# Token mixers with the dense input products issued two k tiles at a time between the lanes' short products

## The chip, the cores and the metric

The kernel runs on one core of a Trainium2 chip. The metric is the device time of one execution in microseconds (us), the median of several. PE stands for the matrix engine (TensorE), DVE for VectorE, ACT for ScalarE, POOL for GpSimd and SP for SyncE, which here only issues transfers.

## What is computed

Two transformer blocks over 512 tokens of width 1024, in float32. The change touches only the first part of the first block, the token mixers. It projects the normed input with one wide matrix and feeds four kinds of mixer, each with a quarter of the width, whose outputs are joined and projected back:

```python
def token_mix(h, w_in, ...):
    p = (h @ w_in).astype(jnp.float32)
    (fox_qkv, fox_f, gdn_qkv, gdn_b, gdn_a, gdn_z, hg_q, hg_f, hg_i, hg_g,
     gla_qk, gla_v, gla_gk, gla_g) = jnp.split(p, _cut_points(IN_SIZES), axis=-1)
    ...
    o_a = rms_norm(fox_attention(q, k, split_heads(v, FOX_HEADS), log_f), fox_on_g)
    ...
    o_b = gated_delta_chunked(...)      # gated delta rule, state carried from chunk to chunk
    ...
    o_c = gla_chunked(...)              # gated linear attention (hg)
    ...
    o_d = gla_chunked(...)              # gated linear attention (gla)
    ...
    return jnp.concatenate([merge_heads(o_a), merge_heads(o_b), merge_heads(o_c), merge_heads(o_d)], axis=-1)

    # first_block
    mixed = token_mix(rms_norm(x, norm1_g[l]), ...)
    x = x + mixed.astype(x.dtype) @ w_out[l]
```

After it come the first block's feed-forward part and the whole second block (a convolution mixer, a SwiGLU, latent attention, a SwiGLU). They are long chains of dense products, and the change doesn't touch their code.

## The kernel before

Activations lie transposed, as eight tiles of 128 features by 512 tokens. Every dense product is done with operands split into a high and a low part: for each k tile three matmuls of 128x128 by 128x512 (high by high, high by low, low by high), eight k tiles to a product. The weights of one product come in by one transfer of 512 KB; ACT makes the high part (line 111) and DVE the low part (line 112, tile `wl`), in two buffers each.

In the mixers there are two kinds of PE work. The **dense products** are 29 tiles of the input projection and 8 of the output projection (tile `mm` in the rows below, all recorded on line 705, the body of the helper `mm`). The **short products** belong to the mixers, which run as three lanes: `gps` (the gated delta rule: gdn0, then gdn1), `lps` (linear attention: hg0, gla, hg1) and `fps` (attention: fox0, fox1). A lane is a chain: a few short matmuls, then DVE, ACT or POOL work on their result, then the next few short matmuls that need it. Transposes are recorded on line 712.

The order in which PE gets all this is written out when the program is built, by `conduct`, which plays the work through on a clock of its own, `self.clk`. Each matmul moves that clock by an assumed cost (`mm`: 0.216 for a dense one, so 0.648 for a k tile). A lane's generator yields how long it wants to wait before its next step; it is due when the clock has passed that time. In each turn `conduct` takes the first lane that is due, unless a dense product is open and more than `FEED` has passed on the clock since the last dense step; else it takes one step of an open dense product:

```python
if due and not (dense and self.clk - fed > FEED):
```

So with lanes always due, short work for just over `FEED` goes by, then a dense step; with none due, dense steps follow each other until one is due. PE runs the finished order from front to back.

A dense product is opened when the one before it has had its last step, and the next one is chosen at that moment, in the order of `ORDER`, among those whose buffers are free. `over` in `mix` says which part of a lane must have been written out before: the products lf1 and lq1 need `la6.qk`, lv1 needs `la6.v` (both parts of the lane step gla), and hg1 can't start before lf1, lq1 and lv1 are there. The output products come when no input product is left. They need the lanes' outputs as k tiles, and those that lack only the last one are parked until it is there (`parked`). Every product ends on DVE (lines 901, 927, 935 for the input, 859 for the output).

Of the kernel before, what the change touches and what calls it, by code (L numbers as in the profile page):

```python
# [20 lines left out]
KD = D // 128  # L21
# [623 lines left out]

LA, LV, LP = 0.68, 1.0, 1.5

FEED = 1.27

# [12 lines left out]
class Mix(Mla):  # L664
# [55 lines left out]
            self.mm(cols(ps[:, cs]), l[:, cs], cols(r[:, cs]))  # L720
        return ps

    def stepped(self, ws, xs, tag):


        ps = (self.pmm if tag == "mm" else self.psm).tile([128, S], F32, tag=tag, name="mm", bufs=2)
        for k in range(KD):
            while k >= len(xs):
                yield None
            self.step(ps, k, ws[xs[k][0]], xs[k])  # L730
            yield ps, k

    def step(self, ps, k, w, x):
        (h, l), (_, xh, xl) = w, x
# [23 lines left out]
    def conduct(self, jobs, lanes):  # L758
# [8 lines left out]
        first, last = jobs.pop(0), []  # L767
        self.last = last
        xs = [(k, *x) for k, x in enumerate(self.xs)]
        nxt, dense, held = (first, self.first), [], []  # L770
        early = [self.second]
        outs, parked, row = list(range(KD)), [], None
        while True:

            for i, lane in enumerate(lanes):
                if strands[i] is None and lane and all(n in ready for n in lane[0][0]):
                    need, name, gen, rings = lane.pop(0)
                    strands[i] = Strand(gen(), max([self.clk] + [ready[n] for n in need]), rings, name)
            live = self.beside + [s for s in strands if s]
            due = next((s for s in live if s.at <= self.clk), None)  # L780

            while held and "mean" in self.over:
                ps, name, post = held.pop(0)
                t = post(ps)
                if t is not None:
                    ready[name] = max(self.clk, ready["mean"] + C_MEAN) + t
            if nxt is None:
                job = next((j for j in jobs if j[1] in self.over), None)
                if job:
                    jobs.remove(job)  # L790
                    nxt = job, early.pop() if early else self.weight(self.a["w_in"], job[0], KD)
                elif not jobs and outs:
                    c = outs.pop(0)
                    nxt = (c, None, None, self.out_post(c)), self.weight(self.a["w_out"], c, KD)
            if not jobs and not held and all(d[1][2] is None for d in dense) and (not nxt or nxt[0][2] is None):
                while self.ended:
                    p = self.ended.pop(0)
                    last.append((p, *self.parts(self.outs[p], "x", KD)))
                    if len(last) == KD:
                        self.load_x(self.a["xT"])  # L800
                        due_row = self.clk + DUE
            if due and not (dense and self.clk - fed > FEED):
                self.lane = due.rings
                t = next(due.gen, None)
                self.lane = {}
                due.at = self.clk + (t or 0.0)
                if t is None:
                    if due in strands:
                        strands[strands.index(due)] = None
                        self.over.add(due.name)  # L810
                        ready[due.name] = self.clk
                    else:
                        self.beside.remove(due)
                continue
            if not row and len(last) == KD - 1 and not any(lanes) and not any(strands):
                row = self.row_of_out(next(i for i in range(KD) if all(x[0] != i for x in last)))
            if parked and len(last) == KD and row and (self.clk > due_row or not (dense or nxt)):
                ps, c, _ = parked.pop(0)
                self.step(ps, KD - 1, row[c], last[KD - 1])
                held.append((ps, None, self.out_post(c)))  # L820
                fed = self.clk
                continue
            tags = ["mm", *self.idle_psum(lanes, live)] if nxt and nxt[0][2] is None else ["mm"]
            taken = [d[2] for d in dense] + [p[2] for p in parked] + ["mm"] * len(held)
            tag = next((t for t in tags if taken.count(t) < 2), None)
            if nxt and tag and len(dense) + len(held) < 2 and all(d[1][2] is None for d in dense):
                job, ws = nxt
                started += 1
                if started in (3, 4):
                    tag = "fps"  # L830
                dense.append((self.stepped(ws, last if job[2] is None else xs, tag), job, tag))
                nxt = None
                continue
            step = None
            for d in dense:
                step = next(d[0])
                if step:
                    break
            fed = self.clk
            if step:  # L840
                ps, k = step
                if d[1][2] is None and k == KD - 2 and len(last) < KD:
                    dense.remove(d)
                    parked.append((ps, d[1][0], d[2]))
                elif k == KD - 1:
                    dense.remove(d)
                    held.append((ps, *d[1][2:]))
                continue
            if not live:
                assert not jobs and not outs and not dense and not any(lanes) and not held  # L850
                return
            self.clk = max(self.clk, min(s.at for s in live))
# [835 lines left out]
```

## Time and profile before

| | us |
|---|---|
| time, median of 3 runs (1859.42 to 1865.12) | 1862.47 |
| the profiled execution's own time | 1862.47 |
| its span, from the first to the last instruction | 1860.8 |
| PE busy | 1822.3 |
| DVE busy | 1050.7 |
| ACT busy | 737.8 |
| POOL busy | 194.4 |

The busy time of PE is a modelled one: its matmuls are pipelined and overlap in the record, so starts of successive instructions tell more than durations. The mixers take the first 400 us of the span; the last matmul on line 705 starts at 399.3 us. In the timeline, rows of one engine stand in order of their starts, with the time that the engine sat idle before in brackets and what ended it.

### The profile page before, as it was taken

To read this page: it belongs to the slowest core of one execution; us is meant where nothing else is said; L and a number is where in the kernel's file an instruction comes from. 1 tells how busy PE (TensorE), PEld (TensorE's weight loads), DVE (VectorE), ACT (ScalarE), POOL (GpSimd) and SP (SyncE) were. 2 spreads that over 40 slices of the span, in tenths; PEclk is the share of its full clock that TensorE was granted. 3 is DMA by queue.
4 is the path that set the end of the run, shared out by engine and by line. 5 is a ranking of instruction groups with operands and counts; after the bars stand their busy time and mean duration, and the time that the engine had idled before them with its cause. 6 is when DMAs were issued, how large, how long until landed. Compare 5 with 4: busy or idle time off the path is not lost.

```text
span 1860.8 us, 22057 instructions
## 1 busy us (share of the span) xinstructions
PE 1822.3 (98%) x8609; PEld 1501.5 (81%) x8609; DVE 1050.7 (56%) x1627; ACT 737.8 (40%) x1138; POOL 194.4 (10%) x225
## 2 busy tenths in 40 slices
PE   8999999999999999999999999999999999999997
PEld 6787887778888888888888888888777888888886
DVE  7875985767777633455564444333876454444323
ACT  6543544544444422322343233322577333232322
POOL 1510502210000001011200000011011200000001
PEclk9999999999999999999999999999999999999999
DMA  4111101332323333323232323333222222323332
GB/s 167 57 35 46 46 35 35 106 101 91 102 93 100 90 100 94 102 91 102 92 106 92 102 91 102 94 94 97 71 60 74 79 96 97 102 91 99 94 94 76
DMA packets 53223, 162.61 MB, mean 87 GB/s; under 512 B 6528, under 2 KB 13184, under 8 KB 53120
## 3 DMA queue, kind: packets, MB, share of 16 engines
q1 hardware_dynamic: 52992, 161.21, 27.2%
q8 instruction: 67, 1.10, 0.3%
q14 instruction: 36, 0.29, 0.0%
q10 hardware_dynamic: 128, 0.01, 0.0%
HBM read 157.78 MB, written 2.10 MB: 86 GB/s over the span
## 4 chain that ended last, share of the span: by engine, by line
PE 85%; DVE 9%; ACT 3%; issue 1%; POOL 1%; DMA 0%; SPq 0%; DVEq 0%; ACTq 0%; POOLq 0%
PE mm L125 24%; PE mm L127 24%; PE mm L126 24%; PE mm L705 6%; PE gps L705 3%; PE lps L705 1%; PE fps L705 1%; DVE lbd L1310 1%; ACT wh L111 1%; DVE wl L112 1%; DVE lat L1361 1%; PE ps L577 1%; DVE ptl L112 0%; PE ps L165 0%; DVE nm L580 0%
## 5 line engine op out<-in xcount | busy, mean ns | idle before, releaser
L111 ACT ACTIVATE wh<-raw 128x1024 fp32r<-128x1024 f32 (+3 forms) x308 | 308.6, 1003 | 762.6 <-PE mm L126 463.5
L125 PE MATMUL mm<-xh,wh 128*128 128x512 f32 x1336 | 521.8, 391 | 0.4 <-ACT xh L173 0.4
L126 PE MATMUL mm<-xl,wh 128*128 128x512 f32 x1336 | 520.7, 390 | 0.5 <-DVE xl L174 0.5
L127 PE MATMUL mm<-xh,wl 128*128 128x512 f32 x1336 | 519.9, 389 | 0.0
L112 DVE TENSOR_TENSOR wl<-raw,wh 128x1024 fp32r<-128x1024 f32 (+3 forms) x300 | 361.0, 1203 | 224.8 <-ACT wh L111 221.6
L126 PEld LDWEIGHTS mm<-xl,wh 128*128 128x128 f32 x1336 | 250.8, 188 | 54.9 <-DVE xl L174 1.4
L125 PEld LDWEIGHTS mm<-xh,wh 128*128 128x128 f32 x1336 | 250.8, 188 | 53.7 <-issue 1.0
L127 PEld LDWEIGHTS mm<-xh,wl 128*128 128x128 f32 x1336 | 250.8, 188 | 51.9 <-issue 0.2
L125 PE MATMUL mm<-hidh,wh 128*128 128x512 f32 (+1 forms) x614 | 236.7, 386 | 0.0
L127 PE MATMUL mm<-hidh,wl 128*128 128x512 f32 (+1 forms) x614 | 235.3, 384 | 0.0
L126 PE MATMUL mm<-hidl,wh 128*128 128x512 f32 (+1 forms) x614 | 233.8, 381 | 0.0
L127 PEld LDWEIGHTS mm<-hidh,wl 128*128 128x128 f32 x614 | 115.4, 188 | 24.2
L126 PEld LDWEIGHTS mm<-hidl,wh 128*128 128x128 f32 x614 | 115.4, 188 | 23.6
L705 PE MATMUL mm<-xh,wh 128*128 128x512 f32 x291 | 127.7, 439 | 6.6 <-ACT xh L173 5.8
L125 PEld LDWEIGHTS mm<-hidh,wh 128*128 128x128 f32 x614 | 115.5, 188 | 21.9 <-ACT wh L111 0.2
L705 PE MATMUL mm<-xh,wl 128*128 128x512 f32 x291 | 116.0, 398 | 1.6 <-DVE wl L112 1.6
L705 PE MATMUL mm<-xl,wh 128*128 128x512 f32 x291 | 116.1, 399 | 0.4 <-DVE xl L112 0.4
L278 DVE TENSOR_TENSOR u<-mm,rb 128x512 f32<-128x512 f32 x44 | 30.4, 691 | 141.2 <-PE mm L127 141.2
L158 POOL TENSOR_TENSOR z<-z,sq 128x512 f32<-128x512 f32 x31 | 50.9, 1643 | 556.6 <-ACT sq L156 518.9
L274 DVE TENSOR_TENSOR u<-mm,rb 128x512 f32<-128x512 f32 x44 | 30.4, 691 | 90.9 <-PE mm L127 90.8
L111 ACT ACTIVATE hidh<-s 128x512 fp32r<-128x512 f32 x66 | 41.8, 633 | 88.6 <-DVE s L255 57.5
L705 PEld LDWEIGHTS mm<-xh,wh 128*128 128x128 f32 x291 | 56.1, 193 | 18.8 <-ACT xh L173 6.3
(434 smaller groups left out, 2089.2 us busy)
## 6 DMA issues: line engine op xcount, KB each, us to landing
raw<-in_w_a_dram SPq DMA_DIRECT2D x52, 512.0 KB, 3.3
raw<-in_w_b_dram SPq DMA_DIRECT2D x52, 512.0 KB, 3.4
raw<-in_w_up_dram SPq DMA_DIRECT2D x44, 512.0 KB, 3.3
raw<-in_w_in_dram SPq DMA_DIRECT2D x28, 512.0 KB, 3.3
raw<-in_conv_w_in_dram SPq DMA_DIRECT2D x24, 512.0 KB, 3.3
raw<-in_w_down_dram SPq DMA_DIRECT2D x16, 448.0 KB, 3.4
raw<-in_w_a_dram SPq DMA_DIRECT2D x16, 448.0 KB, 3.3
raw<-in_w_b_dram SPq DMA_DIRECT2D x16, 448.0 KB, 3.3
```

The costliest lines, as they stand in the source:

```text
L111: nc.scalar.activation(out=h, in_=src, func=ACTF.Copy)
L112: (eng or nc.vector).tensor_tensor(out=l, in0=src, in1=h.bitcast(F32), op=ALU.subtract)
L125: nc.tensor.matmul(out=ps, lhsT=h, rhs=xh, start=(k == 0), stop=False)
L126: nc.tensor.matmul(out=ps, lhsT=h, rhs=xl, start=False, stop=False)
L127: nc.tensor.matmul(out=ps, lhsT=l, rhs=xh, start=False, stop=(k == kt - 1))
L158: eng.tensor_tensor(out=acc, in0=acc, in1=sq, op=ALU.add)
L274: nc.vector.tensor_tensor(out=g, in0=ps, in1=r, op=ALU.mult)
L278: nc.vector.tensor_tensor(out=g, in0=ps, in1=r, op=ALU.mult)
L577: nc.tensor.matmul(out=ps[:, :n], lhsT=l[:, qs], rhs=r[:, :n], start=(i == 0), stop=False)
L705: self.nc.tensor.matmul(out=out, lhsT=lhsT, rhs=rhs, start=start, stop=stop)
L1310: nc.vector.tensor_tensor(out=bd[rows, :, h].rearrange("p c (n j) -> p c n j", j=b), in0=c4(q)[rows], in1=c4(d)[rows], op=ALU.mult)
L1361: nc.vector.copy_predicated(out=at.rearrange("p c (n j) -> p c n j", j=2 * b)[:, :, :, b:], mask=self.lmask[:, lv - 1].rearrange("p (n j) ...
```

## The change

`stepped`, the generator of one dense product, gets a parameter `many`: it hands back control only after every `many`-th k tile. Input products are made with 2, output products keep 1. `FEED` is doubled. What is computed, the number of instructions, buffers and transfers are the same; the order on PE differs, and with it the moments at which products are opened.

```diff
-FEED = 1.27
+FEED = 2.54
...
-    def stepped(self, ws, xs, tag):
+    def stepped(self, ws, xs, tag, many=1):
...
             self.step(ps, k, ws[xs[k][0]], xs[k])
-            yield ps, k
+            if (k + 1) % many == 0 or k == KD - 1:
+                yield ps, k
...
-                dense.append((self.stepped(ws, last if job[2] is None else xs, tag), job, tag))
+                steps = self.stepped(ws, last, tag) if job[2] is None else self.stepped(ws, xs, tag, 2)
+                dense.append((steps, job, tag))
```

## Rows read from the trace of the kernel before

**Rows 1.** The page: span, engines' busy us, and the granted clock by slices.

```profile
span 1860.8 us, 22057 instructions
PE 1822.3 (98%) x8609; PEld 1501.5 (81%) x8609; DVE 1050.7 (56%) x1627; ACT 737.8 (40%) x1138; POOL 194.4 (10%) x225
PEclk9999999999999999999999999999999999999999
```

**Rows 2.** Busy time of each engine by stretch, with granted clock, DMA share and GB/s.

```profile
120.00:180.00 60.00, 59.38 (x362) 48.60 (x361) 34.61 (x87) 22.52 (x55) 5.26 (x11) 1.00 0.11 36
...
240.00:300.00 60.00, 58.37 (x354) 50.27 (x354) 48.12 (x113) 28.88 (x67) 11.35 (x13) 0.94 0.11 36
...
400.00:1860.00 1460.00, 1443.39 (x6515) 1190.26 (x6514) 757.17 (x998) 542.24 (x758) 96.47 (x115) 1.00 0.29 93
```

**Rows 3.** Timeline of PE: start us, us, engine, line, operation, tiles, shapes, count.

```profile
61.77 0.47 PE L705 MATMUL mm<-xh,wh 128*128 128x512 f32 x1
...
83.04 0.48 PE L705 MATMUL mm<-xh,wh 128*128 128x512 f32 x1
...
83.82 0.53 PE L705 MATMUL gps<-gy,gxt 128*128 128x64 f32 x4
84.18 0.62 PE L705 MATMUL gps<-gxt,gy 128*128 128x64 f32 x4
84.62 0.48 PE L705 MATMUL mm<-xh,wh 128*128 128x512 f32 x1
...
86.10 1.05 PE L705 MATMUL lps<-lbd,lw 128*128 128x128 f32 x8
87.12 0.64 PE L705 MATMUL gps<-gy,gxt 128*128 128x64 f32 x4
87.59 0.62 PE L705 MATMUL gps<-gxt,gy 128*128 128x64 f32 x4
...
335.93 0.48 PE L705 MATMUL mm<-xh,wh 128*128 128x512 f32 x1
```

**Rows 4.** Waits of PE from 60 to 400 us: total us, times, longest.

```profile
PE gps L705 <- DVE gxt L1143: 1.9, 4, 0.6
...
PE gps L705 <- ACT gko L1062: 0.2, 1, 0.2
```

**Rows 5.** Busy time by stretch again, of the two with a lower granted clock.

```profile
110.70:114.10 3.40, 3.40 (x11) 2.83 (x11) 3.37 (x6) 1.78 (x2) 0.00 (x0) 0.50 0.00 0
...
291.60:298.40 6.80, 6.80 (x23) 5.51 (x24) 4.73 (x8) 5.70 (x8) 4.59 (x4) 0.50 0.25 78
```

**Rows 6.** Timeline of PE where the clock fell.

```profile
108.75 0.63 PE L705 MATMUL gps<-gy,gxt 128*128 128x64 f32 x4 [0.96 <-DVE gx L1141]
109.75 0.52 PE L705 MATMUL gps<-gxt,gy 128*128 128x64 f32 x3 [0.36 <-DVE gxt L1143]
...
290.36 0.63 PE L705 MATMUL gps<-gy,gxt 128*128 128x64 f32 x4 [0.53 <-DVE gx L1141]
291.60 1.06 PE L705 MATMUL gps<-gxt,gy 128*128 128x64 f32 x4 [0.60 <-DVE gxt L1143]
292.47 0.77 PE L705 MATMUL mm<-xh,wh 128*128 128x512 f32 x1
```

**Rows 7.** Timelines of PE and DVE: the last linear-attention lane's start and end.

```profile
248.20 0.69 DVE L901 TENSOR_TENSOR fv<-mm,rb 128x512 f32<-128x512 f32 x1 [0.31 <-PE mm L705]
...
276.81 0.69 DVE L901 TENSOR_TENSOR lf<-mm,rb 128x512 f32<-128x512 f32 x1 [0.35 <-PE mm L705]
...
314.76 0.69 DVE L901 TENSOR_TENSOR lv<-mm,rb 128x512 f32<-128x512 f32 x1
...
316.06 0.61 PE L712 MATMUL lps<-mlac,lv 128*128 128x128 f32 x4
...
379.18 0.60 PE L712 MATMUL lps<-mlac,s 128*128 128x128 f32 x4
```

**Rows 8.** Line 705 by tiles: duration ns min/median/max, first and last start us, forms.

```profile
L705 PE MATMUL mm<-xh,wl x291: 387/393/632, 7.2 to 399.3; 128*128 128x512 f32 x146
```

## The prediction

> **What bounds the kernel now.** I read the page first. PE is busy for 1822.3 of 1860.8 us [rows 1], so everything hangs on PE. But that busy time is modelled, and it doesn't tell stages apart. So the busy times by stretch come next. Behind 400 us the code is untouched and PE holds its full clock for 1460 us [rows 2]; I take that part over as it is. All that can move lies in the first 400 us, the mixers, where the clock is at 1.00 in some stretches and at 0.94 in another [rows 2]. There the timeline of PE shows how dense steps (`mm`) and short groups alternate [rows 3], the list of waits shows what PE stood still for [rows 4], and the stretches with a lower clock [rows 5] and what stood ahead of them [rows 6] show the rest.
>
> The reader should see a small pool. The change alters the order of PE's instructions, not their number. PE's idle time between 60 and 400 us comes to 10.0 us in eleven kinds, 15 times in all, from 1.9 us down to 0.2 us (the first and the last of them stand in [rows 4]). The clock stands at 0.50, 1.2 GHz, for 3.4 and for 6.8 us [rows 5], which costs half of that, 5.1 us. An order without any fault could therefore win 15 us, 0.8%, and an order that switches more cheaply a little beside. The other direction has no such bound.
>
> **The change part by part.** The profiled execution took 1862.47 us, exactly the median of the runs shown, with a span of 1860.8 us; sums are made on 1862.5.
>
> **Fewer, longer dense bursts.** Between 60 and 340 us I count 102 bursts of dense steps: 61 of a single k tile (the first at 61.77, the last at 335.93), 36 of two (as at 84.62), five longer [rows 3]. So many are pairs already. A single one takes 0.78 us to the next group (83.04 to 83.82), a pair 1.48 us (84.62 to 86.10) [rows 3]. Two singles made one pair save 1.56 - 1.48 = 0.08 us. That looks like 30 x 0.08 = 2.4 us for the 61 singles. But the short groups pay it back. The group gps<-gy,gxt of four takes 0.36 us where it follows a dense step (83.82 to 84.18; 15 places alike) and 0.47 us where it follows another short group (87.12 to 87.59; the middle of nine places is 0.45) [rows 3]. A merge makes one short group follow a short group instead of a dense step: +0.09. What a switch costs is a cost behind every short group, whatever follows. Bounds: -2.4 us if the short groups pay nothing, +0.3 us if each pays 0.09. I take 0, since the most frequent kind of group shows the payment.
>
> **The feed threshold.** While lanes are always due, short work runs until the planner's clock has passed `FEED`. By `mm` a lane's step counts 0.32 (four of 0.08) up to 1.73 (eight of 0.216), so the threshold is overshot by about 0.45. Before, 0.648 of dense work came for 1.72 of short, 27%; after, 1.296 for 2.99, 30%. Input products go about a tenth faster there and lanes 4% slower. That costs nothing while both kinds are there to fill PE. Output products, with `many` at 1, get half the rate while a lane is due, which also costs nothing as long as the lane fills PE.
>
> **Waits on the lanes.** Where no lane is due at first, a lane that becomes due inside a pair is served up to one k tile (0.70 us, 1.48 - 0.78) later. Its DVE result is older by then, and waits get shorter. Where lanes press, the opposite holds: of two dense steps that lay between short groups one is gone from its place. A lane's matmul whose DVE result isn't there stops PE, and the dense steps queued behind it, on which nothing is missing, wait with it: the group at 291.60 stood idle for 0.60 us, and the dense step behind it began at 292.47 [rows 6]. The trace of before doesn't show such places after the change. Bounds: -10.0 us (every wait gone [rows 4]), and +23 us (30 merges, each uncovering a whole 0.78 us). I take 0, nearest to the pattern of [rows 3], where short groups already stand three in a row (86.10, 87.12, 87.59) without an idle mark; cover is moved from one gap to the next, not removed.
>
> The page "TensorE: Matmul & The Clock Gate" of the Trainium skill says in Part 2 that only weight loads are pulled ahead and that matmuls stay in program order. The trace agrees (292.47 behind 291.60), and this rule speaks against the change.
>
> **Granted clock.** Both falls to 1.2 GHz came right behind two waits on the same lane: 0.96 and 0.36 us ahead of the first, 0.53 and 0.60 us ahead of the second [rows 6]. A new order can lose these two (-5.1 us) or have another like the longer (+3.4 us). I take 0. Single dense steps alone don't bring the clock down: 120 to 180 us holds many and is at 1.00 [rows 2].
>
> The page "Perfetto Trace Analysis" of the Trainium skill, section Matmul Optimizations, says that the engine scales its power with utilization, so that matmuls should run back to back in batches. By that rule pairs should keep the clock up and the 5.1 us would be won; the trace shows the falls behind waits and not behind singles, so the rule has no term in the sum.
>
> **The tail.** hg1 is the last lane. It begins at 316.06, right behind the end of its last input product (lv1, at 314.76), and its last transposes stand at 379.18 [rows 7]. The last dense matmul of the mixers starts at 399.3 [rows 8], 20 us behind that. Of that, the code makes at least the last k tiles of six parked products and two whole products wait for hg1: 6 + 16 = 22 steps of 0.70, 15.4 us. So about 5 us of slack cover a later end of hg1. Cost 0, and with that cover gone each us later is a us lost.
>
> **Transfers and splits.** SP's weight loads, ACT's and DVE's splits and the evacuations keep number and size. They move only with the moments at which products open, a k tile or two. Nothing is moved past another kind of work. Cost 0.
>
> Sum: 1862.5 + 0 + 0 + 0 + 0 + 0 = 1862.5 us.
>
> **The rivals.** A, slower: PE waits more. At the 30 places where a dense step leaves its gap, the lane's result comes too late by half a step: 30 x 0.39 = 11.7 us, 1874 us; with one more fall of the clock 1878. It decides from about 14 such places on (14 x 0.39 = 5.5 us). For it: the planner counts a float32 group of eight as 1.73, while it takes at most 1.02 us (86.10 to 87.12 [rows 3]), so a lane that looks due after 1.0 on that clock has had less time in truth, and without a dense step between nothing makes it up. Against it: three lanes take turns.
>
> B, faster: the two pairs of waits (1.32 and 1.13 us [rows 6]) and both falls (5.1 us [rows 5]) vanish because PE has two k tiles of cover at these places: 7.5 us, 1855.0 us; if short groups don't pay back the 2.4 us, 1852.6. For it: both places had a single step or a pair just behind which the lane wasn't ready. Against it: other such places can arise.
>
> C, slower: hg1 starts one product later. Products are chosen when the one before has ended. lf1, which hg1 needs, was chosen about 248.2, when fv1 ended [rows 7], and became free (la6.qk) only shortly before. If lanes are 4% slower by then, the choice misses it and another product goes first. From lf1's end to lv1's end two products take 38 us (276.81 to 314.76 [rows 7]), 19 each. 19, less 5 for faster products, less 5 of slack, is 9 us: 1872. Against it: the moments of choice move too, and may fall as well.
>
> D: it hardly does what it says, as pairs were there already and output products stay single: 1862, no change.
>
> **How the numbers follow.** A measurement of this kernel can tell about 0.3%, 5.6 us. Forecast (no change) 0.50, D 0.05, A 0.17, C 0.11, B 0.17. Within 0.3%: 0.55. Slower: A and C, 0.28. Faster: B, 0.17. The range goes from 1854 (B, short of its end) to 1875 (C and A, short of A's end), and leaves out some 0.07 below and 0.1 above; the likeliest case by itself spans 1857 to 1868.
>
> **What would show it.** Right, step by step: far fewer single bursts and about 70 to 85 bursts in place of 102; a pair still at 1.48 us and gps<-gy,gxt still at 0.36 and 0.45; waits of PE between 60 and 400 us within 5 us of 10.0; one to three falls of the clock; hg1's last transposes before about 384; from the mixers' end on the same length as before. Wrong: waits above 20 us would be A, waits near 3 us with no fall B, lv1's end behind 325 us C, single bursts as many as before D.

## The result, and the profile after

The changed kernel took 1885.63 us (median of four executions, 1879.77 to 1892.15), the kernel before, run beside it, 1863.24 us. The ratio is 1.0128, with an interval of 1.0111 to 1.0145: slower by 1.3%, where no change was forecast and the range ended at 1875. One execution of the kernel e1 further down took 3070.01 us at a mean granted clock of 0.554, against 0.981 to 0.988 in the others, and is left out of its row.

The page of after: span, engines' busy us, and the granted clock in 40 slices.

```profile
span 1888.6 us, 22059 instructions
PE 1838.6 (97%) x8609; PEld 1516.4 (80%) x8609; DVE 1051.1 (56%) x1627; ACT 739.5 (39%) x1138; POOL 193.0 (10%) x225
PEclk9999997999999999999999999999999999999999
```

The counts of PE's, DVE's, ACT's and POOL's instructions are those of [rows 1], and DVE and ACT are as busy as before. New is the 7 in PEclk. To see which part of the span grew, take the row of the first matmul behind the mixers: its first and last start, before and then after.

```profile
L125 PE MATMUL mm<-xh,wh x1336: 387/389/799, 399.5 to 1725.6; 128*128 128x512 f32 x191
```

```profile
L125 PE MATMUL mm<-xh,wh x1336: 387/389/799, 429.6 to 1753.5; 128*128 128x512 f32 x191
```

The mixers end 30.1 us later (399.5 to 429.6). From there to the span's end it is 1461.3 us before and 1459.0 after. So the whole loss lies in the mixers. Next, busy time by stretch: length, busy PE, PEld, DVE, ACT, POOL, then granted clock. Before, then after:

```profile
60.00:400.00 340.00, 329.74 (x1888) 273.55 (x1887) 247.03 (x533) 154.98 (x311) 88.65 (x88) 0.98 0.17 54
```

```profile
60.00:430.00 370.00, 346.66 (x1885) 288.89 (x1884) 249.46 (x534) 156.53 (x311) 87.31 (x88) 0.93 0.16 51
120.00:180.00 60.00, 58.63 (x373) 49.65 (x372) 31.08 (x72) 20.78 (x50) 4.73 (x9) 1.00 0.11 37
240.00:300.00 60.00, 59.80 (x364) 51.13 (x363) 51.45 (x129) 30.78 (x66) 10.35 (x12) 1.00 0.11 36
303.10:333.80 30.70, 30.34 (x106) 25.21 (x107) 10.35 (x23) 8.04 (x21) 2.14 (x2) 0.50 0.08 27
340.00:400.00 60.00, 52.84 (x308) 44.48 (x308) 38.44 (x86) 23.44 (x44) 11.47 (x12) 0.94 0.21 66
430.00:1888.00 1458.00, 1442.75 (x6515) 1190.17 (x6514) 755.15 (x996) 541.67 (x757) 96.24 (x115) 1.00 0.29 93
```

Two things are read here. PE stood for 340 - 329.74 = 10.3 us before and for 370 - 346.66 = 23.3 us after: 13 us more. And the clock: 0.93 instead of 0.98. Neither is spread evenly: 120 to 180 and 240 to 300 us are about as full as before (58.63 and 59.80 us of PE against 59.38 and 58.37) and at 1.00 (before: 1.00 and 0.94 [rows 2]), while 340 to 400 holds 52.84 at 0.94. One stretch, 303.1 to 333.8, ran at 1.2 GHz throughout, although PE was busy for 30.34 of its 30.70 us. In all, the mixers of after hold 51.1 us at 1.2 GHz (3.4 from 74.4, 6.8 from 108.6, 3.4 from 224.6, 30.7 from 303.1, 3.4 from 368.0, 3.4 from 391.9), those of before 10.2 [rows 5]. Half of the 40.9 more is lost, by estimate 20.4 us. 13.2 and 20.4 make 33.6 against a measured 30.1 us. The sum counts idle time at the low clock one and a half times, but that is only 1.05 us of idle in after, 0.5 us too much; the other 3 us are looked at below the table of the experiments.

The four executions of after differ by the clock alone, as far as can be seen: at a mean granted clock of 0.984 and 0.985 they took 1890.35 and 1892.15 us, at 0.990 and 0.989 1879.77 and 1880.91. A difference of 0.005 over 1885 us is 9.4 us, and the two pairs lie 10.9 us apart. So the profiled execution is one of the two that stayed long at 1.2 GHz, and the median holds some 5 us less of that.

PE's waits of after between 60 and 430 us (us in total, times, longest):

```profile
PE gps L705 <- DVE gx L1143: 4.4, 2, 3.5
PE fps L705 <- ACT fpt L1477: 3.7, 1, 3.7
PE gps L705 <- ACT gko L1064: 3.1, 1, 3.1
PE gps L705 <- DVE gst L1204: 2.4, 1, 2.4
PE gps L705 <- ACT gmt L1090: 1.5, 1, 1.5
...
PE mm L705 <- DVE xl L112: 0.2, 1, 0.2
```

It isn't many small waits, as rival A had it: 18 waits in all, of which the four longest hold 12.6 of the 23.3 us. What the engine waited for was doing meanwhile stands in its own timeline. The longest, on PE:

```profile
296.41 0.44 PE L712 MATMUL fps<-mlac,fp 128*128 128x128 f32 x2
...
299.18 0.61 PE L705 MATMUL gps<-gxt,gy 128*128 128x64 f32 x4
303.45 1.12 PE L705 MATMUL fps<-fv,fpt 128*128 128x64 f32 x4 [3.66 <-ACT fpt L1477]
304.33 0.77 PE L705 MATMUL mm<-xh,wh 128*128 128x512 f32 x1
```

On ACT in after, and then on ACT and PE at the place of before where the same work of ACT stands (there the copy belongs to the attention lane's next unit, 128x384):

```profile
298.72 1.04 ACT L111 ACTIVATE wh<-raw 128x1024 fp32r<-128x1024 f32 x1
299.78 1.28 ACT L261 ACT_TABLE_LOAD   x1
301.08 0.63 ACT L261 ACTIVATE lq<-lq 128x512 f32<-128x512 f32 x1
301.72 1.28 ACT L264 ACT_TABLE_LOAD   x1
303.02 0.38 ACT L1477 ACTIVATE fpt<-fps 128x256 f32<-128x256 f32 x1
```

```profile
291.37 1.05 ACT L111 ACTIVATE wh<-raw 128x1024 fp32r<-128x1024 f32 x1
292.44 1.28 ACT L261 ACT_TABLE_LOAD   x1
293.73 0.63 ACT L261 ACTIVATE lq<-lq 128x512 f32<-128x512 f32 x1
294.27 0.61 ACT L261 ACTIVATE gate<-gate 128x512 f32<-128x512 f32 x1
294.90 1.28 ACT L264 ACT_TABLE_LOAD   x1
296.19 0.49 ACT L1475 ACTIVATE fpt<-fps 128x384 f32<-128x384 f32 x1
```

```profile
293.90 0.84 PE L712 MATMUL fps<-mlac,fp 128*128 128x128 f32 x3
```

`fpt` is a copy of 0.38 us. The transposes that it reads had left PE by 296.85, but it ran at 303.02: in ACT's order it stood behind steps of linear attention, for one of which ACT itself sat idle before 298.40, and behind a weight split, a table load, an activation and a second table load (298.72 to 303.0). While ACT works these off, PE stands, with the dense step of 304.33 queued behind it. In before the same split and two table loads stand in front of `fpt`, and PE doesn't wait: it issues the transposes only at 293.90, in the middle of that work, and has other work, part of it at 1.2 GHz, up to the group that reads `fpt` at 298.75. So the table loads as such weren't new; the moment at which the lane met them was. The second longest wait, at 109.07 on PE, and DVE's work ahead of it:

```profile
103.53 0.61 PE L705 MATMUL gps<-gxt,gy 128*128 128x64 f32 x4
...
105.22 0.40 PE L705 MATMUL mm<-xh,wl 128*128 128x512 f32 x1
109.07 1.06 PE L705 MATMUL gps<-gy,gxt 128*128 128x64 f32 x4 [3.45 <-DVE gx L1143]
...
112.50 0.77 PE L705 MATMUL mm<-xh,wh 128*128 128x512 f32 x1
```

```profile
104.42 1.01 DVE L143 SCALAR_TENSOR_TENSOR sq<-sq 128x512 f32<-128x512 f32 x1
...
105.69 0.68 DVE L145 SCALAR_TENSOR_TENSOR sq<-sq 128x512 f32<-128x512 f32 x1
...
106.63 1.50 DVE L1444 SCALAR_TENSOR_TENSOR fk<-rk,mixp,sq 64x512 f32<-64x512 f32 x2
108.14 0.42 DVE L1312 TENSOR_TENSOR lbd<-lq,s 64x256 f32<-64x256 f32 x1
108.59 0.42 DVE L1143 TENSOR_TENSOR gx<-gx,gps 128x256 fp32r<-128x256 f32 x1
```

`gx` is a step of 0.42 us of the delta-rule lane (gdn). The group that it reads ended by 104.14 on PE, but until 108.59 DVE worked through the preparation of q and k of the attention lane (fox: `sq`, `fk`) and through steps of linear attention (`lat`, `lbd`), without a gap. Before, the same place costs 0.96 and 0.36 us [rows 6]. The next two waits are alike: `gko` (PE stood 3.06 us) ran 2.9 us after the transposes that it reads, `gst` (2.38 us) 1.8 us after its product. So in the four longest waits of after PE waits for a short step whose input is there and which lacks only its turn in another engine's queue. The other 14 hold 10.8 us and aren't all of this kind: at 389.81 PE stood 1.5 us for ACT's split `xh` of a lane's output, and ACT itself had sat idle for that output.

### The profile page after: what moved, and what is told of

It is laid out like the page before. It is cut to its first block, busy times and chain, and to the rows that moved or that the text cites. A ratio compares the mean times of both kernels' runs of the same rounds, so it can differ in the third digit from the quotient of the medians.

```text
span 1888.6 us, 22059 instructions
## 1 busy us (share of the span) xinstructions
PE 1838.6 (97%) x8609; PEld 1516.4 (80%) x8609; DVE 1051.1 (56%) x1627; ACT 739.5 (39%) x1138; POOL 193.0 (10%) x225
## 4 chain that ended last, share of the span: by engine, by line
PE 86%; DVE 7%; ACT 4%; issue 1%; POOL 1%; DMA 0%; DVEq 0%; SPq 0%; POOLq 0%; ACTq 0%
PE mm L125 24%; PE mm L127 24%; PE mm L126 24%; PE mm L705 7%; PE gps L705 3%; PE lps L705 2%; PE fps L705 1%; ACT wh L111 1%; DVE lbd L1312 1%; POOL s L1301 1%; DVE wl L112 1%; PE ps L577 0%; DVE lat L1363 0%; DVE ptl L112 0%; PE ps L165 0%
## 5 line engine op out<-in xcount | busy, mean ns | idle before, releaser
L125 PEld LDWEIGHTS mm<-hidh,wh 128*128 128x128 f32 x614 | 115.5, 188 | 21.9 <-ACT wh L111 0.2
```

Source lines behind the costliest of these rows:

```text
L125: nc.tensor.matmul(out=ps, lhsT=h, rhs=xh, start=(k == 0), stop=False)
```

## The experiments

All figures in one table. Idle is PE's idle time from 60 us to the mixers' end; low is the time that the mixers spend at 1.2 GHz; both, and the mixers' end, are from the trace of each kernel's profiled execution. Us throughout.

| kernel | median | before beside it | ratio (interval) | mixers' end | idle | low |
|---|---|---|---|---|---|---|
| before | 1863.24 | | | 399.5 | 10.1 | 10.2 |
| after | 1885.63 | 1863.24 | 1.0128 (1.0111 to 1.0145) | 429.6 | 23.3 | 51.1 |
| e1_pairs_only | 1897.58 | 1861.21 | 1.0178 (1.0146 to 1.0209) | 437.9 | 28.2 | 64.9 |
| e2_feed_only | 1875.76 | 1861.21 | 1.0071 (1.0046 to 1.0096) | 421.4 | 20.9 | 30.6 |
| e5_fours | 1899.89 | 1861.21 | 1.0202 (1.0185 to 1.0219) | 438.4 | 22.4 | 75.0 |
| e3_feed_1_35 | 1862.37 | 1861.21 | 1.0005 (0.9994 to 1.0017) | 400.0 | 10.3 | 10.2 |
| e6_feed_1_15 | 1870.71 | 1862.92 | 1.0034 (1.0015 to 1.0052) | 404.7 | 12.9 | 17.0 |
| e7_feed_0_64 | 1895.04 | 1860.39 | 1.0183 (1.0162 to 1.0204) | 426.9 | 21.6 | 34.1 |
| e18_before_gdn_3_later | 1894.23 | 1864.34 | 1.0156 (1.0131 to 1.0182) | 435.5 | 24.0 | 54.5 |
| e19_before_fox_3_later | 1876.57 | 1864.34 | 1.0068 (1.0052 to 1.0083) | 416.6 | 19.5 | 27.2 |
| e20_after_gdn_3_later | 1884.59 | 1864.34 | 1.0112 (1.0097 to 1.0128) | 417.3 | 25.2 | 17.0 |
| e21_after_fox_3_later | 1892.18 | 1862.50 | 1.0159 (1.0126 to 1.0193) | 434.6 | 29.7 | 51.1 |
| e8_after_f32_half | 1896.79 | 1860.39 | 1.0191 (1.0174 to 1.0207) | 436.0 | 27.6 | 54.5 |
| e15_after_longer_yields | 1915.82 | 1862.92 | 1.0277 (1.0258 to 1.0296) | 453.6 | 32.8 | 85.2 |
| e13_after_no_low | 1889.98 | 1862.92 | 1.0135 (1.0103 to 1.0167) | 434.7 | 25.2 | 68.2 |
| e14_before_no_low | 1865.91 | 1862.92 | 1.0015 (1.0003 to 1.0028) | 404.7 | 14.4 | 13.6 |
| e11_after_wl_pool | 1906.89 | 1860.39 | 1.0258 (1.0223 to 1.0294) | 457.2 | 33.8 | 85.2 |
| e10_before_one_wait | 1870.73 | 1860.39 | 1.0054 (1.0036 to 1.0071) | 405.4 | 15.2 | 13.6 |
| e17_after_fq_pool | 1876.37 | 1864.34 | 1.0065 (1.0048 to 1.0083) | 421.2 | 22.7 | 34.1 |
| e22_before_fq_pool | 1859.06 | 1862.50 | 0.9984 (0.9972 to 0.9995) | 396.2 | 8.7 | 6.8 |

In the profiled execution of e7 the granted clock was 0.95 from 12 us on; its last column holds only the time at 1.2 GHz.

Read the last three columns together: by (idle - 10.1) + (low - 10.2) / 2 the mixers of e2 should end 21.0 us later, and they end 21.9 later; e18 36.1 and 36.0; e19 17.9 and 17.1; e22 -3.1 and -3.3. In e7, with its lower clock throughout, the sum of 23.5 is too small against 27.4. With pairs and fours it is too large: after 33.6 and 30.1, e13 44.1 and 35.2, the worst. Idle time at the low clock, which is counted one and a half times, explains only part of that (in after 0.5 us, in e13 5.45 us of idle at 1.2 GHz, so 2.7). Without it the kernels with single k tiles lie within 1.5 us of the sum on either side (e7 aside), those with pairs 2.0 to 4.6 us below it (only e20 lies 0.6 above), and e5, with fours, 4.5 below. So waits and the clock account for the loss; longer bursts cost nothing by themselves and seem to make PE's own work some 3 us shorter. That is a remainder of modelled busy times, and no run takes it alone.

### One part of the change alone, and more of it

e1 has the pairs without the threshold (in after), e2 the threshold without the pairs (in before, with a line that lets the planner's clock run on where only parked output products are left), e5 fours.

```
-FEED = 2.54
+FEED = 1.27                                       # e1
-FEED = 1.27
+FEED = 2.54                                       # e2
-... else self.stepped(ws, xs, tag, 2)
+... else self.stepped(ws, xs, tag, 4)             # e5, with FEED = 5.08
```

> Input products in pairs of k tiles, FEED left at 1.27. Three theories of the loss of 22 us. Portion: it is the pairs, since a lane that comes due waits for two k tiles and its work on DVE and ACT comes later and in clumps; this run then loses as much as the whole change, 1875 to 1890. Feed: it is the longer run of short steps allowed by the doubled threshold; this run then stays within 6 us of before (1863). Phase: neither as such, but any new order shifts where a lane's step meets a busy DVE or ACT queue, and PE stands still there, until the clock falls; this run then loses anything from 5 to 30 us.

> One k tile at a time as before, FEED doubled to 2.54 (with a mend in the planner for the case that all that is left waits for the last output tile). Portion: within 6 us of before. Feed: the whole loss, 1875 to 1890. Phase: a loss of 5 to 30 us here too, with no relation to that of the pairs alone.

> Input products in fours of k tiles with FEED at 5.08, the same change once more in the same direction. Portion and Feed: the loss grows with the step, at least twice that of the change, 1905 or more, with more waits of PE than the change has. Phase: no order by size, between 1868 and 1895.

Either part alone loses, e1 36 us, more than both together, e2 15, somewhat less, and fours lose 39 us, not twice the 22 of pairs. The parts don't add, so neither can be given a share of the loss. Portion and Feed had each expected one of the two to stay within 6 us of before, and neither did; Phase had the sign, but its 30 us (e1) and 1895 (e5) were passed.

### Does any other order lose?

e3, e6 and e7 are before with only the threshold changed, to 1.35, 1.15 and 0.64; 65, 355 and 1199 lines of the list of PE's instructions then stand in another place. e18 and e19 leave `many` and `FEED` as before and start one lane later, by 3.0 on the planner's clock (both with the line of e2); e20 and e21 do the same in after.

```
-FEED = 1.27
+FEED = 1.35                                       # e3; 1.15 in e6, 0.64 in e7
-        yield 0.0
+        yield 3.0                                 # e18, e20: first step of gdn
-            yield LA
+            yield 3.0 + LA                        # e19, e21: first step of fox
```

> The kernel before with FEED at 1.35 in place of 1.27: the smallest change of order, single k tiles throughout. Portion and Feed: no loss to speak of, 1858 to 1868. Phase: may lose 5 us and more, with waits of PE at places where before has none.

> The kernel before with FEED at 1.15: an order of PE that differs at 355 lines, between the nudge to 1.35 (65 lines, no loss) and the new orders (1000 to 1350 lines, 13 to 38 us lost). If a loss grows with how much of the order is new: 1863 to 1875. If the threshold's direction decides (a smaller one mixes finer): 1858 to 1863.

> Single k tiles with FEED at 0.64, half of that of before: dense and short work mixed more finely, with an order of PE that differs from that of before at 1199 lines, about as many as that of the change (1346). Phase (any new order loses): 1870 to 1890. Clumping (longer stretches of short steps, or of dense steps, make the lanes' work reach DVE and ACT in clumps, so that PE, which takes everything in order, stands behind a backlog): a finer mix has no more waits than before, idle time of PE from 60 us to the mixers' end 6 to 12 us, and a time of 1855 to 1866.

> The kernel before, portions and threshold as they were; the gated delta lane begins each time 3.0 later on the planner's clock. PE's order differs at 1275 lines. Phase (where lanes meet on DVE and ACT decides, and a new order deals this anew): 1866 to 1890, idle time of PE from 60 us on 13 to 25 us. Portion (single k tiles keep lanes supplied): within 6 us of before.

> The same with the attention lanes, each half of whose preparation begins 3.0 later on the planner's clock; 776 lines of PE's order differ from before. Phase: 1866 to 1890, and not the same as with the gated delta lane. Portion: within 6 us of before.

> The changed kernel with the gated delta lane 3.0 later. Phase: anything between 1865 and 1905, below or above the change (1885), with other waits at other places. Portion: 1880 to 1895, as the pairs are the same.

> The changed kernel with the attention lanes' preparation 3.0 later on the planner's clock. Phase: somewhere between 1868 and 1905, not tied to the change's 1885, with idle time of PE and time at 1.2 GHz that explain it to within 8 us. Portion: 1880 to 1895.

These speak most clearly. e18 feeds as before and still has mostly single bursts, 63 of them between 60 and 400 us against 61; it loses 30 us, more than the change. From 60 to 436 us:

```profile
60.00:436.00 376.00, 351.84 (x1893) 290.18 (x1892) 258.97 (x542) 156.87 (x312) 86.25 (x88) 0.93 0.15 50
```

24 us idle and a clock of 0.93, just as in after. e7 feeds finer than before and loses 35 us (in the profiled execution the mixers end 27 us later, and some 9 us more are lost behind them, where its granted clock is 0.95 too). e3, with 65 lines moved, loses nothing, e6, with 355, 8 us; 776 lines (e19) 12 us. So every order run that shifts the lanes far against each other loses, with singles and with pairs. With singles it was 12 to 35 us (e19, e2, e18, e7), with pairs 20 to 53 (e20, after, e21, e1, e8, e15). Whether pairs bring more waits than singles can't be told from so few orders. The sizes weren't foreseen: e18 and e7 lie above the 1890 that Phase had allowed. Portion is out: e18 and e19 have single k tiles and were to stay within 6 us of before. Clumping is out with e7, whose finer mix was to have no more waits. Before's order has the fewest waits of those run; why just this one isn't shown.

### Is it what the planner believes?

e8 halves its price for float32 matmuls in after, since rival A rested on eight counting as 1.73 for at most 1.02 us [rows 3]. e15 lets each lane rest longer behind a step.

```
-        self.clk += max(1.69e-3 * n, 0.2) if ...
+        self.clk += max(0.845e-3 * n, 0.1) if ... # e8
-LA, LV, LP = 0.68, 1.0, 1.5
+LA, LV, LP = 0.9, 1.5, 2.0                        # e15
```

> The changed kernel, with the planner's cost of a float32 short matmul halved (to what the trace shows for groups of eight). Miscount (the waits come because the planner counts these groups twice as long as they are and so serves lanes too early): the waits mostly go, 1862 to 1872. Clumping: the portions stay at two k tiles and the threshold at 2.54, which then lets even more short work pass; the loss stays at 15 to 35 us.

> The changed kernel with the planner's latencies of lanes (LA, LV, LP) raised from 0.68, 1.0 and 1.5 to 0.9, 1.5 and 2.0, so that lanes are served later. If PE's waits come from lanes served too early: idle time falls below 15 us and the time to 1865 to 1878, until the lanes' later end costs it back. If they come from the moments at which lanes and weights coincide on DVE and ACT: other waits of the same sum, 1875 to 1900.

Both are slower than after, and idle rises to 27.6 and 32.8 us. If lanes were served too early by a constant bit, and that were the bulk of the waits, both should have shortened them. But both deal a new order as well, and an order far from before's cost 12 us and more above. So that reason of rival A isn't borne out, and it isn't ruled out as a part.

### Is it DVE's load?

e13 and e14 leave out the low part of the 27 input weights, in after and in before: DVE's subtraction goes, ACT's copy stays. e11 gives that subtraction to POOL in after.

```
-... self.weight(self.a["w_in"], job[0], KD)
+... self.weight(self.a["w_in"], job[0], KD, low=False)           # e13, e14
+... self.weight(self.a["w_in"], job[0], KD, eng=self.nc.gpsimd)  # e11
```

> The changed kernel with PE's order untouched; the low parts of the weights of 27 input products are left out on DVE (the third matmul of a k tile takes the high part again, so PE has the same work, and the low part of these weights is missing from the result). DVE is rid of 27 x 1.23 = 33 us of work. Queue (PE stands in order behind results that lie in a DVE or ACT queue behind other lanes' and the weights' work): idle time of PE in the mixers falls from 23 us to 15 or less, the clock falls less, and the time comes to 1862 to 1878. Chain (a lane's own latency is too long for its place in the order): within 6 us of the change, 1880 to 1890.

> The same omission in the kernel before (low part of 27 input products' weights left out, PE's order and work as before). Queue: its 10 us of idle time shrink too, but there is little to win, 1850 to 1860. Chain: no change, 1858 to 1866. The distance to the changed kernel with the same omission says how much of the 22 us hangs on DVE's load.

> The changed kernel with PE's order untouched; the low parts of the weights of 27 input products are made by POOL in place of DVE, which takes some 33 us of work off DVE's queue. Clumping, with DVE's backlog as what PE stands behind: waits of PE on DVE fall, and the time by 5 to 20 us, to 1866 to 1880. If the waits are set by the lanes' own chains, with no queue in them: as the change, 1880 to 1890, or slower for the slower split on POOL.

DVE loses a tenth of its work in e13, and the waits stay. The stretch, and the place of the 3.45 us:

```profile
60.00:430.00 370.00, 344.68 (x1854) 287.49 (x1853) 224.50 (x506) 149.71 (x299) 81.53 (x85) 0.91 0.14 49
```

```profile
109.59 1.06 PE L709 MATMUL gps<-gy,gxt 128*128 128x64 f32 x4 [3.82 <-DVE gx L1147]
```

DVE is busy for 224.50 us instead of 249.46, and PE waits 3.82 us for `gx` instead of 3.45. The subtraction wasn't among the steps that stood in front of `gx`; what counts there isn't how much DVE has to do in all but what stands in front of the step that PE needs next. By its expectation this run spoke for Chain, a lane's own latency; the four waits above, whose steps ran 1.8 to 6.2 us after their input was there, speak against that. Less work in before even cost 3 us (e14): two new waits, 3.8 us on ACT's `lv` and 2.6 on ACT's `gko`, came with it. With the subtraction on POOL, e11, where one takes 2.4 us, idle rises to 33.8 us. The longest wait is 7.2 us, on ACT's `gko` near 258 us, and the moved step stands in its chain: on POOL the subtraction (from 252.92, 2.34 us) lies ahead of `s` of linear attention, ACT sits idle for that `s` for 2.93 us, and `gko` comes behind it in ACT's order. Moving work off DVE had only put it into another queue.

### What one wait costs

e10 adds seven copies on ACT behind one evacuation of the attention lane in before; PE's order stays.

```
+            if p == 1 and u == 4:
+                for _ in range(7):
+                    nc.scalar.activation(out=pt[:, :n], in_=tp[:, :n], func=ACTF.Copy)
```

> The kernel before with seven more copies of the same values by ACT at one place (fox1, fifth unit, near 285 us), so that one short group comes late by about 3 us and nothing else changes. It prices a single wait. Wait alone: 2 to 4 us more than before (1864 to 1866). Wait and clock: the clock falls behind it and stays at 1.2 GHz for 3 to 30 us, so that the run loses 5 to 15 us, most of it in dense steps and short groups that take twice as long.

PE's timeline at that place, and the stretch behind 299.9 us by busy time and clock:

```profile
297.08 0.40 PE L705 MATMUL mm<-xh,wl 128*128 128x512 f32 x1
302.67 1.54 PE L705 MATMUL fps<-fv,fpt 128*128 128x64 f32 x6 [5.20 <-ACT fpt L1478]
```

```profile
299.90:306.70 6.80, 4.03 (x17) 3.83 (x18) 0.56 (x1) 2.77 (x7) 0.17 (x1) 0.50 0.00 0
```

One wait of 5.20 us, longer than the 3 that were meant, made the mixers end 5.9 us later; the clock fell while PE still stood and was low for 6.8 us. The wait isn't given back later: PE has no slack. The kernel's median is 10 us above before's, the profiled execution 5.7, so the other executions lost more, which no trace here shows.

### Moving the heavy step out of the way

e17 (after) and e22 (before) take fox's q and k scaling, the `fq` and `fk` in front of `gx`, from DVE to POOL and ACT. PE's order stays in both.

```
+            nc.gpsimd.tensor_tensor(out=raw, in0=raw, in1=rr, op=ALU.mult)
...
-                nc.vector.scalar_tensor_tensor(
-                    out=aug[t, j][0:64], in0=raw[rows], scalar=gain[rows], in1=rr[rows], ...
-                )
+                nc.scalar.activation(out=aug[t, j][0:64], in_=raw[rows], func=ACTF.Copy, scale=gain[rows])
```

> The changed kernel with PE's order untouched; the scaling of the attention lanes' queries and keys goes from DVE (eight of 0.75 us in the mixers) to POOL and ACT. In the changed kernel PE stands 3.45 us near 109 us for gx, while DVE works through the attention lane's preparation. Heavy step in front (the wait is the work of another lane's heavy step that lies ahead in the same queue): that wait falls to 2 us or less, and the time by 1 to 6 us. If the wait has another source: that wait stays.

> The kernel before, PE's order untouched, with the scaling of the attention lanes' queries and keys on POOL and ACT in place of DVE. Before, PE stands 0.96 and 0.36 us behind gx near 109 us, and the clock falls there for 3.4 us. If the heavy step in front is the cause, both go: 1 to 4 us less, 1857 to 1861. If not: within 1 us of before, or slower for the longer way over POOL.

In after the wait at 109 shrank from 3.45 to 2.64 us, less than expected, as `sq`, `lat` and `lbd` still stand there. The kernel is 9 us faster than after, more than the 1 to 6 expected; idle fell by only 0.6 us, and in the profiled executions the gain is in the clock: at 301 it stayed at 1.2 GHz for 17.1 instead of 30.7 us. That needn't be this edit's doing, as after's own executions differ by as much. In before the waits at this place go altogether:

```profile
107.81 0.39 PE L705 MATMUL mm<-xh,wl 128*128 128x512 f32 x1
108.03 0.53 PE L705 MATMUL gps<-gy,gxt 128*128 128x64 f32 x4
```

The 0.96 and 0.36 us of [rows 6] are gone. The fall at 110.7 isn't there either, and 6.8 us at 1.2 GHz are left, at 288.7. But that fall can't be put down to the two waits: e10, whose edit lies far behind, has both waits at the same place, and its clock stays up (e3 is alike).

```profile
108.91 0.63 PE L705 MATMUL gps<-gy,gxt 128*128 128x64 f32 x4 [0.95 <-DVE gx L1141]
...
110.70:114.10 3.40, 3.40 (x21) 2.79 (x19) 3.37 (x6) 1.78 (x2) 0.00 (x0) 1.00 0.00 0
```

So the waits repeat from execution to execution, and the falls behind short ones don't always. The mixers of e22 end at 396.2, and the kernel takes 1859.06 us, by the ratio 0.16% less than before: small, but the interval ends below 1, and it is the fastest of all that ran.

## Why the prediction was wrong

**Bursts: right in what happens, a little too high in cost.** 74 bursts between 60 and 340 us instead of 102, 70 of them pairs; a pair 82.83 to 84.30, and the group behind it 0.36 us, as in [rows 3]:

```profile
82.83 0.48 PE L705 MATMUL mm<-xh,wh 128*128 128x512 f32 x1
...
84.30 0.54 PE L705 MATMUL gps<-gx,gmr 128*128 128x64 f32 x4
84.66 0.47 PE L705 MATMUL mm<-xh,wh 128*128 128x512 f32 x1
...
322.96 1.06 PE L712 MATMUL lps<-mlac,lv 128*128 128x128 f32 x4
...
404.52 0.60 PE L712 MATMUL lps<-mlac,s 128*128 128x128 f32 x4
404.87 0.47 PE L705 MATMUL mm<-xh,wh 128*128 128x512 f32 x1
```

gps<-gy,gxt took 0.36 us behind a dense step and 0.45 behind a short one, as before. But not every kind of short group pays that: gps<-gk of eight (64x128) took 1.08 or 1.09 us behind a dense step and behind a short one alike. The remainder of some 3 us under the table of the experiments says that the term was nearer to its bound of -2.4 than to 0. D fell.

**Tail and transfers: right in cost.** hg1 began at 322.96 and ended at 404.52, behind the 384 that was named. But 24.7 us of dense work (404.87 to 429.6) were left then, against 20 before, so its end bound nothing. It began 6.9 us later than before and took 18.5 us longer, of which some 13 are 4.3 us more of waits and half of the 17.6 us that it ran at 1.2 GHz. The product lv1 ended at 319.8, not behind the 325 of rival C, which fell. The splits were not quite free, as the 1.5 us at 389.81 show.

**Waits on the lanes: the first step that failed.** The 0 was taken from the nearest pattern, short groups that stand three in a row without an idle mark [rows 3], on the ground that cover is moved and not removed. That pattern shows lanes that meet nothing. The measured term is +13.2 us, inside the bounds of -10 to +23, and above the 20 us of idle that were named as the mark of A. What the step left out: a lane's step has its place in two queues, PE's and DVE's or ACT's. The planner's clock counts only what PE does; in the other engines a step runs when its turn comes, and a new order puts other work in front of it. In the four longest waits of after the step that PE needed ran 1.8 to 6.2 us after its input was there. "Moved" was therefore not neutral: of the other orders run only the one nearest to before's had as few waits.

The page "TensorE: Matmul & The Clock Gate" of the Trainium skill, Part 2, has matmuls stay in program order. The trace agrees again: the dense step at 304.33 came behind the group that had waited for 3.66 us.

**Granted clock: the second, and the larger.** It was taken at 0, with one more fall (3.4 us lost) as its worst. Measured: 51.1 us at 1.2 GHz in six stretches, of which one lasted 30.7 us, by estimate 20.4 us more lost than before. That falls come with waits was right: each of the six begins within 2.1 us of the end of one of 1.5 us or more. That a wait brings a fall wasn't: in before three single waits longer than those in front of the falls, of 1.73, 1.53 and 1.15 us (at 352.53, 64.24 and 238.42), had none behind them. But the bound took one more fall of a length seen in before, when waits three times as long were allowed for in the step above; the two terms had to be priced together. And nothing in before showed a stay of 30.7 us.

The page "Perfetto Trace Analysis" of the Trainium skill, section Matmul Optimizations, says that the engine scales its power with utilization and asks for matmuls back to back in batches. Here larger batches came with more time at 1.2 GHz (51.1 us for pairs, 75.0 for fours, 10.2 for before), and singles in another order with 54.5 (e18): the size of the batch alone doesn't decide it.

**Rivals.** A had the sign and the place, not the mechanism: 30 waits of 0.39 us were not found, but a few of 1 to 4 us, and its 1878 had 3.4 us for the clock where some 20 were lost. Its reason, the planner's price of float32, wasn't borne out by e8. B fell.

**Open.** Why the clock came back after 3.4 us at most places and after 30.7 us at 303 isn't settled; PE was busy in both, and two executions of after lost about 10 us less. Which waits bring a fall isn't settled either. Whether pairs bring more waits than singles is open too, and so is how many of the 14 smaller waits come from a queue and how many from a lane's own chain.

## What to carry to other kernels

Where one engine runs lanes in an order written out beforehand, a reorder that neither adds nor removes work isn't free: price it by what each step will stand behind in the other engines' queues. Shift one lane a little in the kernel before, too: what that costs gives a measure of what a new order as such may cost, whatever the idea behind it. Price a wait together with the granted clock behind it. And look for gains in the queue that a wait comes from (e22: a heavy step moved off DVE, PE's order kept) before the order itself.

## What was not expected of the hardware

TensorE stayed at 1.2 GHz for 30.7 us while it was busy for 30.34 of them (17.1 us with 16.70 busy in e17), with dense 128x512 steps among short groups. And in one execution, that of e7, the granted clock was 0.95 from 12 us on, also over the 1290 us from 600 us, where PE was busy for 1281.03. The time doesn't follow that figure in full: from the mixers' end to the span's end it is 1470.1 us against 1461.3 before, 0.6% more and not 5%.

```profile
600.00:1890.00 1290.00, 1281.03 (x5780) 1054.14 (x5778) 627.97 (x833) 463.40 (x661) 91.62 (x84) 0.95 0.28 91
```
